# A block sum by accumulating DMA in the 7-product steps, in place of VectorE's add

## The chip, the cores and the metric

The kernel runs on one core of one Trainium2 chip. The metric is the device time of one execution in microseconds (us), median of several runs; smaller is better. A core has five engines with instruction streams of their own, each in order: TensorE (PE in the profile, its weight loads PEld), VectorE (DVE), ScalarE (ACT), GpSimd (POOL) and SyncE (SP). They meet only at semaphores. DMA transfers are issued by SP, ACT or POOL and carried out by 16 DMA engines.

## The reference

One layer of a hybrid block on x of 256 tokens by 4096 channels, all in float32. One input projection feeds two branches, sparse attention and a state-space mixer; each is projected back to 4096 channels, weighed by a sigmoid gate, summed, sent through an output projection, normalized and added to x. Cut to what matters:

```python
h = rms_norm(x, pre_norm_gain[layer])
proj = h @ w_in[layer]                      # 4096 x 24704
...
y_a = attn.reshape(b, s, ATTN_WIDTH) * jax.nn.silu(gate_a)
y_b = ssd_mixer(xs, z, bm, cm, dt_raw, ...)
gates = jax.nn.sigmoid(merge_logits.astype(jnp.float32)).reshape(b, s, N_BRANCHES, D_MODEL)
merged = (gates[:, :, 0, :] * (y_a @ w_branch_attn[layer])
          + gates[:, :, 1, :] * (y_b @ w_branch_ssd[layer]))
out = merged.astype(x.dtype) @ w_out[layer]
x = x + rms_norm(out, post_norm_gain[layer])
```

Nearly all work is in the matrix products with w_in, the two branch weights and w_out.

## The kernel before

**Float32 by three products.** Weights and activations are split into a rounded part and a rest (wh and wl, copy by ACT at L485, rest by VectorE at L487 or L489; both in `split`). `product` (L525) makes three matmuls of 128x128 by 128x512 (L532): rest times high, high times rest, high times high.

**Column pairs.** Most of the products run in `pair_gemm` (L514): two blocks of 512 output columns by two blocks of 128 tokens, over 4096 (or for the branches 2 x 2048) input channels in 16 steps of 256. A step loads 4 blocks of 128x512 weights in two raw tiles of two blocks each, ra and rb. A step of kind "S" computes its 2x2 block product with 7 products in place of 8 (Winograd's form), for which it needs sums and differences of the weight blocks; a step of kind "D" or "R" makes the 8 products. Which steps are S is set by the tables SX, SS, SY, SM: some 6 or 7 of 16. There are 172 S steps in all.

**One S step, before.** VectorE adds a block of rb to a block of ra (L580). `split(rb, 2)` gives b11, b21; `split(ra, 2)` gives t1 (the sum) and b22. VectorE then overwrites a block of ra with t2 (L585) and rb with t3, t4 (L586), and those are split too. ACT's copy and VectorE's rest of every tile alternate.

**What sets the order.** The program is written step by step; a scheduler puts each engine's instructions into an order by program position and its own estimate of times, so an instruction of a later step may stand ahead of one of an earlier step on the same engine. Raw tiles come from a pool of 8 (RBUFS), so the loads of a step wait until the tiles of the step four before it are free. wh and wl have 5 tiles each. Between the products, `step` (L106) lets generators in `aux` go on: evacuations of the pair before, attention, the state-space mixer, the forms of the next activations.

**The queues.** SP issues all weight loads (`load_half`, L145) and the loads of gates (sg, L1044). POOL issues 54 stores to scratch in DRAM: yscr (outputs of the two mixers, L763 and L946, 8 each), sscr (gates, L994, 32) and mscr (merged blocks, L1076, 6); and 28 loads of them as fr (L1001, L1006). ACT issues none.

The names: raw_N are the raw tiles, wh_N and wl_N the split parts, fr the reloaded activations, sg the reloaded gates, pc a pair's output in SBUF, p the PSUM banks.

Of the kernel before, what the change touches and what calls it, by code (L numbers as in the profile page):

```python
# [19 lines left out]
S = 256  # L20
# [14 lines left out]
SS = (1, 5, 8, 10, 12, 14)  # L35
SY = (1, 4, 6, 9, 12, 14)
SM = SX
GATES = [((n, br), (n + 1, br)) for n in (0, 2, 4, 6) for br in range(2)]
ISCALE = 32 ** -0.5 * 64 ** -0.5

# [5 lines left out]
def fused_block(tc, x, xT, w_qi, w_misc, w_q0, w_qk, w_vg, w_x, w_z, w_gate, w_br, w_out2, w_out,  # L46
# [467 lines left out]
    def pair_gemm(what, mode, chunk, plan, outs, evac, hooks={}, pace=1):  # L514
# [53 lines left out]

        after = max([n for n, (_, kind) in enumerate(plan) if kind == "S"], default=-2) + 1
        ended = []  # L570
        for n, (i, kind) in enumerate(plan):
            ra, rb = raw_tile(), raw_tile()
            load_half(ra, chunk(i), 0)
            load_half(rb, chunk(i), 1)
            if n in hooks:
                hooks[n]()
            assert kind_of[i] == what, (n, i, kind_of, len(aux))
            assert kind == "R" or ext_n[i] == {"S": 4, "D": 2}[kind], (n, i, ext_n)
            if kind == "S":
                V.tensor_add(ra[:, 0, :], ra[:, 0, :], rb[:, 0, :])  # L580
                b11, b21 = split(rb, 2)
                t1, b22 = split(ra, 2)
                if n == 1:
                    run_pending()
                V.tensor_sub(ra[:, 1, :], ra[:, 0, :], ra[:, 1, :])  # L585
                V.tensor_sub(rb, rb, ra[:, 1:2, :].to_broadcast([P, 2, NW]))  # L586
                t2, = split(ra[:, 1:2, :], 1)
                t3, t4 = split(rb, 2)
                now = {1: ("A11", b11), 2: ("A12", b21), 3: ("S4", b22), 4: ("A22", t4),
                       5: ("S1", t1), 6: ("S2", t2), 7: ("S3", t3)}  # L590
                for j in (2, 5, 3, 1, 6, 7, 4):
                    product(j, i, *now[j])
            else:
                w = {}
                w[1, 2], w[2, 2] = split(ra, 2, -1)
                w[1, 1], w[2, 1] = split(rb, 2)
                if n == 0 and len(pending) > 1 and turned[0] == "aux":
                    pending.pop(0)()
                if n == 1:
                    run_pending()  # L600
                if n == after:
                    early()
                    if not left.get(5):
                        late()
                        ended.append(5)
                if n == len(plan) - 1 and dest and not ended and left.get(8) == 0:
                    V.scalar_tensor_tensor(dest[3], dest[2], -1.0, ps[8], ALU.mult, ALU.subtract)
                    ended.append(8)
                todo = [(k, j) for j in ((5, 3, 2, 4) if kind == "D" else (3, 8, 2, 4))
                        for k in (1, 2)]  # L610
                for k, j in todo:
                    name = {2: f"A1{k}", 4: f"A2{k}", 8: f"A2{k}", 5: f"A2{k}",
                            3: f"D{k}" if kind == "D" else f"A1{k}"}[j]
                    product(j, i, name, w[k, 1 if j in (2, 4) else 2])
                    if (k, j) == todo[3]:
                        step(pace)
            step(pace)
# [82 lines left out]
    def attend(j, c):  # L700
# [59 lines left out]
            part(u)  # L760
            yield
        for i in range(2):
            nc.gpsimd.dma_start(yscr[2 * j + i], yraw[i].rearrange("p k t -> p (k t)"))  # L763

    push(make_rstd())
    for j in range(2):
# [156 lines left out]
    def finish(g, yvt):  # L923
        yv = [yvt[:, t, :] for t in range(2)]
        z = zs[g // 4]
        s2 = ssdp.tile([P, 2], F32, tag="ys2", name="ys2")
        for t in range(2):
            V.tensor_mul(yv[t], yv[t], z[2 * t + g % 4 // 2][:, g % 2 * S:g % 2 * S + S])
            sq = ssdp.tile([P, S], F32, tag="cacc", name="sq")
            A.activation(sq, yv[t], AF.Square, accum_out=s2[:, t:t + 1])  # L930
        ry = ssdp.tile([P, 2], F32, tag="yry", name="yry")
        rsqrt(ry, s2, 1.0 / S, ssdp)
        yield
        for t in range(2):
            A.activation(yv[t], yv[t], AF.Copy, scale=ry[:, t:t + 1])
        yield
        b = aux_bank().rearrange("p (c k) -> p c k", c=2)
        for c in range(2):
            for t in range(2):
                T.transpose(b[:, c, t * P:(t + 1) * P], yv[t][:, c * P:(c + 1) * P], ident)  # L940
        yb = ssdp.tile([P, 2, S], F32, tag="xd", name="yb")
        for c in range(2):
            k = 2 * g + c
            A.activation(yb[:, c, :], b[:, c, :], AF.Copy,
                         scale=pc[:, PC_NG + k:PC_NG + k + 1])
        nc.gpsimd.dma_start(yscr[8 + g], yb.rearrange("p k t -> p (k t)"))  # L946
        yield

    def ev_x(m):
# [39 lines left out]
    def ev_gate(cols):  # L989
        def run(c):  # L990
            for q, o in enumerate(c):
                t, (n, br) = q // 2, cols[q % 2]
                A.activation(o, o, AF.Sigmoid, scale=rstd[:, t:t + 1])
                nc.gpsimd.dma_start(sscr[br, n, t], o)  # L994
                if q % 2:
                    yield
        return run
# [48 lines left out]
    def ev_branch(n, br):  # L1046
        def run(c):
# [14 lines left out]
            for b in range(2):  # L1062
# [10 lines left out]
                    transpose4(c[2 * t + b], mT[:, :, t * P:(t + 1) * P], A)  # L1073
                    yield
                if n < 6:
                    nc.gpsimd.dma_start(mscr[n + b], mT.rearrange("p k t -> p (k t)"))  # L1076
                else:
                    for h in range(2):
                        merged[2 * (n + b) + h] = mT[:, 2 * h:2 * h + 2, :]
# [240 lines left out]
```

## Time and profile before

| | |
|---|---|
| median of 3 runs | 2861.69 us (2857.63 to 2864.1) |
| profiled execution, span from first to last instruction | 2848.7 us |
| median less span | 13.0 us |
| L580, the add in question | 172 times, 118.7 us |
| granted TensorE clock, mean | 0.996 |

The profiled execution is known by its span; its own device time isn't listed. The profile page gives busy time by engine, groups of instructions by line, and DMA issues. A row of a group reads: line, engine, operation, written tile <- read tiles, shapes, count | busy us, mean ns of one | idle us of the engine just before them, and what ended it. A row of the timeline reads: start us, length us, engine, line, operation, tiles, shape, count, and in brackets the idle time before it and what ended it. A "q" behind an engine's name means its instruction queue.

### The profile page before, as it was taken

Reading aid. Unit: us, or ns where it says so; the run is one execution under the profiler, and the core shown is the slowest. Engines: PE = TensorE matmul, PEld = TensorE weight load, DVE = VectorE, ACT = ScalarE, POOL = GpSimd, SP = SyncE. Lnnn points to the kernel's source line nnn. Section 1 sums busy time; section 2 is a strip of 40 time slices with the busy share of each in tenths; the row PEclk is TensorE's granted clock in tenths of the full one; section 3 lists DMA queues with packets and bytes.
Section 4 is the critical chain, followed back from the end, with each engine's and each line's share of the span. In section 5 each row is a group of like instructions: output and inputs, shape, how many; then the busy total and the mean of one; then the engine's idle time right before and its main releaser. Section 6 shows DMA issues by size and latency. Waiting matters only on the chain.

```text
span 2848.7 us, 35818 instructions
## 1 busy us (share of the span) xinstructions
PE 2813.4 (99%) x12744; PEld 2316.0 (81%) x12744; DVE 2407.6 (85%) x3039; ACT 1686.4 (59%) x2208; POOL 60.3 (2%) x98
## 2 busy tenths in 40 slices
PE   9999999999999999999999999999999999999997
PEld 7877888888888888888887788888887888888886
DVE  6668988989889878988898788988887899988875
ACT  7444565555656656876788555555555555555552
POOL 0100000000000000000000000000000000000000
PEclk9999999999999999999999999999999999999999
DMA  9544565655555555555555666666676676866673
GB/s 370 190 159 167 186 202 180 205 192 201 195 188 199 192 200 199 175 184 193 182 190 175 212 219 217 225 217 214 217 240 230 233 236 225 287 205 206 230 252 132
DMA packets 170852, 592.41 MB, mean 208 GB/s; under 512 B 19633, under 2 KB 20401, under 8 KB 170673
## 3 DMA queue, kind: packets, MB, share of 16 engines
q1 hardware_dynamic: 163728, 567.05, 58.6%
q0 software_dynamic: 6944, 23.07, 2.3%
q8 instruction: 100, 1.64, 0.2%
q14 instruction: 80, 0.65, 0.1%
HBM read 570.12 MB, written 19.92 MB: 207 GB/s over the span
## 4 chain that ended last, share of the span: by engine, by line
PE 55%; issue 35%; DVE 5%; DMA 3%; POOL 1%; ACT 0%; SPq 0%; POOLq 0%; DVEq 0%; ACTq 0%
PE p L532 43%; PE p L192 3%; PE p L193 3%; PE p L194 3%; DVE wl L489 1%; DVE wl L184 1%; PE p L362 1%; DMA fr<-yscr 1%; DMA raw<-w_out_d 1%; POOL sscr L994 0%; DMA raw<-w_qk_d 0%; DMA raw<-w_z_d 0%; PE p L393 0%; PE p L745 0%; DVE wl L487 0%
## 5 line engine op out<-in xcount | busy, mean ns | idle before, releaser
L485 ACT ACTIVATE wh<-raw 128x1024 fp32r<-128x1024 f32 (+1 forms) x1240 | 1186.3, 996 | 799.3 <-DVE raw L585 397.4
L532 PE MATMUL p<-wh,b 128*128 128x512 f32 x4504 | 1513.2, 393 | 3.6 <-ACT wh L485 1.8
L489 DVE TENSOR_TENSOR wl<-raw,wh 128x1024 fp32r<-128x1024 f32 (+1 forms) x964 | 1065.1, 1126 | 132.5 <-ACT wh L485 130.2
L532 PEld LDWEIGHTS p<-wh,b 128*128 128x128 f32 x4504 | 847.2, 188 | 179.1 <-ACT wh L485 4.1
L532 PE MATMUL p<-wl,b 128*128 128x512 f32 x2252 | 879.4, 391 | 6.1 <-DVE wl L489 3.8
L532 PE MATMUL p<-wh,ext 128*128 128x512 f32 x2320 | 810.5, 390 | 0.9 <-ACT wh L485 0.9
L532 PEld LDWEIGHTS p<-wh,ext 128*128 128x128 f32 x2320 | 435.6, 188 | 92.1 <-ACT wh L485 2.1
L532 PEld LDWEIGHTS p<-wl,b 128*128 128x128 f32 x2252 | 424.1, 188 | 93.6 <-DVE wl L487 4.8
L532 PE MATMUL p<-wl,ext 128*128 128x512 f32 x1160 | 452.7, 390 | 1.6 <-DVE wl L489 1.6
L487 DVE SCALAR_TENSOR_TENSOR wl<-raw,wh 128x1024 fp32r<-128x1024 f32 x276 | 337.0, 1221 | 48.0 <-ACT wh L485 47.7
L532 PEld LDWEIGHTS p<-wl,ext 128*128 128x128 f32 x1160 | 217.8, 188 | 50.9 <-DVE wl L489 5.7
L586 DVE TENSOR_TENSOR raw<-raw 128x1024 f32<-128x1024 f32 x172 | 210.5, 1224 | 3.8
L184 DVE TENSOR_TENSOR wl<-raw,wh 128x1024 fp32r<-128x1024 f32 x112 | 138.8, 1241 | 85.4 <-ACT wh L183 83.8
L192 PE MATMUL p<-wh,b 128*128 128x512 f32 x512 | 202.1, 396 | 1.7 <-ACT wh L180 1.7
L193 PE MATMUL p<-wl,b 128*128 128x512 f32 x512 | 200.1, 391 | 0.0
L194 PE MATMUL p<-wh,b 128*128 128x512 f32 x512 | 199.9, 391 | 0.0
L183 ACT ACTIVATE wh<-raw 128x1024 fp32r<-128x1024 f32 x112 | 118.4, 1060 | 131.1 <-PE p L194 118.4
L580 DVE TENSOR_TENSOR raw<-raw 128x512 f32<-128x512 f32 x172 | 118.7, 690 | 88.8 <-DMA raw<-w_gate_d 35.1
L585 DVE TENSOR_TENSOR raw<-raw 128x512 f32<-128x512 f32 x172 | 118.5, 689 | 2.3
L192 PEld LDWEIGHTS p<-wh,b 128*128 128x128 f32 x512 | 96.3, 188 | 26.0 <-ACT wh L180 3.3
L194 PEld LDWEIGHTS p<-wh,b 128*128 128x128 f32 x512 | 96.5, 189 | 20.4
L193 PEld LDWEIGHTS p<-wl,b 128*128 128x128 f32 x512 | 96.6, 189 | 19.9 <-DVE wl L181 0.4
(236 smaller groups left out, 1366.5 us busy)
## 6 DMA issues: line engine op xcount, KB each, us to landing
raw<-w_gate_d SPq DMA_DIRECT2D x256, 512.0 KB, 4.7
raw<-w_vg_d SPq DMA_DIRECT2D x128, 512.0 KB, 4.3
raw<-w_x_d SPq DMA_DIRECT2D x128, 512.0 KB, 4.3
raw<-w_br_d SPq DMA_DIRECT2D x128, 512.0 KB, 4.8
raw<-w_out_d SPq DMA_DIRECT2D x128, 512.0 KB, 4.7
raw<-w_qk_d SPq DMA_DIRECT2D x96, 512.0 KB, 4.5
raw<-w_z_d SPq DMA_DIRECT2D x64, 512.0 KB, 4.6
raw<-w_qi_d SPq DMA_DIRECT2D x62, 512.0 KB, 6.0
```

The lines of the kernel that those rows point to most:

```text
L183: A.activation(wh, rs, AF.Copy)
L184: V.tensor_sub(wl, rs, wh.bitcast(F32))
L192: T.matmul(ps[t], al[:, tk], wh[:, i, :], start=first, stop=False)
L193: T.matmul(ps[t], ah[:, tk], wl[:, i, :], start=False, stop=False)
L194: T.matmul(ps[t], ah[:, tk], wh[:, i, :], start=False, stop=last)
L485: A.activation(h, src, AF.Copy, scale=float(sign))
L487: V.scalar_tensor_tensor(l, src, -1.0, fbit(h), ALU.mult, ALU.subtract)
L489: V.tensor_sub(l, src, fbit(h))
L532: T.matmul(ps[j], l, r, start=first and n == 0, stop=left[j] == 0 and n == 2)
L580: V.tensor_add(ra[:, 0, :], ra[:, 0, :], rb[:, 0, :])
L585: V.tensor_sub(ra[:, 1, :], ra[:, 0, :], ra[:, 1, :])
L586: V.tensor_sub(rb, rb, ra[:, 1:2, :].to_broadcast([P, 2, NW]))
```

## The change

It takes the add out of VectorE and lets a DMA add: once ra is loaded, POOL issues a DMA that reads the block (the first block of rb) from DRAM a second time and accumulates it into ra. For this the loads of a step are written two steps ahead of its work (`fetch`, LEAD = 2). The stores of yscr, sscr and mscr move from POOL's queue to ACT's. Products and splits stay.

```diff
+LEAD = 2
...
-        for n, (i, kind) in enumerate(plan):
+        loaded = deque()
+
+        def fetch(n):
+            i, kind = plan[n]
             ra, rb = raw_tile(), raw_tile()
             load_half(ra, chunk(i), 0)
             load_half(rb, chunk(i), 1)
+            if kind == "S":
+                nc.gpsimd.dma_start(ra[:, 0, :], chunk(i)[:, HK, :], accum_op=ALU.add)
+            loaded.append((ra, rb))
+
+        for n in range(LEAD):
+            fetch(n)
+        for n, (i, kind) in enumerate(plan):
+            if n + LEAD < len(plan):
+                fetch(n + LEAD)
+            ra, rb = loaded.popleft()
...
             if kind == "S":
-                V.tensor_add(ra[:, 0, :], ra[:, 0, :], rb[:, 0, :])
                 b11, b21 = split(rb, 2)
                 t1, b22 = split(ra, 2)
...
-            nc.gpsimd.dma_start(yscr[2 * j + i], yraw[i].rearrange("p k t -> p (k t)"))
+            nc.scalar.dma_start(yscr[2 * j + i], yraw[i].rearrange("p k t -> p (k t)"))
...
-        nc.gpsimd.dma_start(yscr[8 + g], yb.rearrange("p k t -> p (k t)"))
+        nc.scalar.dma_start(yscr[8 + g], yb.rearrange("p k t -> p (k t)"))
...
-                nc.gpsimd.dma_start(sscr[br, n, t], o)
+                nc.scalar.dma_start(sscr[br, n, t], o)
...
-                    nc.gpsimd.dma_start(mscr[n + b], mT.rearrange("p k t -> p (k t)"))
+                    nc.scalar.dma_start(mscr[n + b], mT.rearrange("p k t -> p (k t)"))
```

The change moves instructions beyond these lines, since the scheduler orders anew. VectorE before, in the second gate pair; raw_13981 and raw_13982 belong to a D step, raw_14017 and raw_14018 to the S step after it, raw_14061 and raw_14062 to the next D step, raw_14097 and raw_14098 to the S step after that:

```order
L580 TENSOR_TENSOR raw_14097<-raw_14097,raw_14098 128x512
L489 TENSOR_TENSOR wl_13990<-raw_13982,wh_13989 128x1024
L489 TENSOR_TENSOR wl_14023<-raw_14018,wh_14022 128x1024
L489 TENSOR_TENSOR wl_14027<-raw_14017,wh_14026 128x1024
L585 TENSOR_TENSOR raw_14017<-raw_14017 128x512
L586 TENSOR_TENSOR raw_14018<-raw_14018,raw_14017 128x1024
L489 TENSOR_TENSOR wl_14033<-raw_14017,wh_14032 128x512
L489 TENSOR_TENSOR wl_14037<-raw_14018,wh_14036 128x1024
L487 SCALAR_TENSOR_TENSOR wl_14066<-raw_14061,wh_14065 128x1024
L489 TENSOR_TENSOR wl_14070<-raw_14062,wh_14069 128x1024
L489 TENSOR_TENSOR wl_14103<-raw_14098,wh_14102 128x1024
L489 TENSOR_TENSOR wl_14107<-raw_14097,wh_14106 128x1024
```

The add of one S step stands eleven rows ahead of the split of its sum, in front of the rest of three earlier steps. The same place of VectorE now (the tiles have other numbers: the two D steps are raw_13901, raw_13902 and raw_13990, raw_13991, the two S steps raw_13946, raw_13947 and raw_14026, raw_14027):

```order
L490 TENSOR_TENSOR wl_13999<-raw_13902,wh_13998 128x1024
L490 TENSOR_TENSOR wl_14032<-raw_13947,wh_14031 128x1024
L490 TENSOR_TENSOR wl_14036<-raw_13946,wh_14035 128x1024
L598 TENSOR_TENSOR raw_13946<-raw_13946 128x512
L599 TENSOR_TENSOR raw_13947<-raw_13947,raw_13946 128x1024
L490 TENSOR_TENSOR wl_14042<-raw_13946,wh_14041 128x512
L490 TENSOR_TENSOR wl_14046<-raw_13947,wh_14045 128x1024
L488 SCALAR_TENSOR_TENSOR wl_14075<-raw_13990,wh_14074 128x1024
L490 TENSOR_TENSOR wl_14079<-raw_13991,wh_14078 128x1024
L490 TENSOR_TENSOR wl_14112<-raw_14027,wh_14111 128x1024
L490 TENSOR_TENSOR wl_14116<-raw_14026,wh_14115 128x1024
```

The adds are gone, and VectorE's rows now follow the steps one after the other. POOL before, around the end of the state-space mixer (yb are its outputs, pc the gates):

```order
L994 DMA sscr_110<-pc_13454 128x512
L994 DMA sscr_110<-pc_13456 128x512
L946 DMA yscr_108<-yb_13844 128x512
L1001 DMA fr_17767<-yscr_108 128x512
L1001 DMA fr_17769<-yscr_108 128x512
L994 DMA sscr_110<-pc_14236 128x512
L994 DMA sscr_110<-pc_14233 128x512
```

and POOL now, at the same place:

```order
L580 DMA raw_13856<-w_gate_d 128x512
L580 DMA raw_13946<-w_gate_d 128x512
L1014 DMA fr_17776<-yscr_108 128x512
L1014 DMA fr_17778<-yscr_108 128x512
L580 DMA raw_14026<-w_gate_d 128x512
L580 DMA raw_14106<-w_gate_d 128x512
```

The stores have left, and accumulates stand before and behind the two loads of yscr. ACT now, at the head of a gate pair, with the stores among the gates' sigmoids (L1006) and the copies of the raw tiles (L486); before, its row held the four sigmoids one behind the other and no store:

```order
L1006 ACTIVATE pc_14899<-pc_14899,rstd_98 128x512
L1006 ACTIVATE pc_14897<-pc_14897,rstd_98 128x512
L1007 DMA sscr_110<-pc_14899 128x512
L1006 ACTIVATE pc_14896<-pc_14896,rstd_98 128x512
L486 ACTIVATE wh_14996<-raw_14931 128x512
L1007 DMA sscr_110<-pc_14896 128x512
L486 ACTIVATE wh_15000<-raw_14932 128x1024
L1007 DMA sscr_110<-pc_14897 128x512
```

Every store stands one to five rows behind the sigmoid that it stores.

## The prediction

> **What bounds the kernel now.** I read the page's busy times first, then the chain that ended last, then a table of stretches, then the groups of TensorE (PE), and last the timeline at the places where PE stood still.
>
> ```profile
> span 2848.7 us, 35818 instructions
> PE 2813.4 (99%) x12744; PEld 2316.0 (81%) x12744; DVE 2407.6 (85%) x3039; ACT 1686.4 (59%) x2208; POOL 60.3 (2%) x98
> ...
> PE 55%; issue 35%; DVE 5%; DMA 3%; POOL 1%; ACT 0%; SPq 0%; POOLq 0%; DVEq 0%; ACTq 0%
> ```
>
> PE is busy for 2813.4 of 2848.7 us, and the change removes no product. So the whole gain must come out of 35.3 us in which PE stands still. VectorE (DVE) at 85% is not the bound on the average; only where it is late for a moment does PE wait for it. The table of stretches tells where PE stands still (first number the length, second PE's busy time, fourth VectorE's, the fraction near the end the DMA engines' busy share):
>
> ```profile
> 290.00:1090.00 800.00, 797.68 (x3638) 659.68 (x3638) 703.44 (x830) 463.34 (x583) 4.46 (x8) 1.00 0.58 196
> 1090.00:1253.00 163.00, 162.43 (x761) 133.83 (x760) 144.22 (x208) 126.47 (x202) 1.09 (x2) 1.00 0.53 179
> 1253.00:1330.00 77.00, 75.16 (x343) 60.36 (x342) 65.96 (x98) 59.34 (x94) 1.09 (x2) 1.00 0.56 189
> 1330.00:1500.00 170.00, 169.58 (x780) 139.25 (x779) 151.97 (x206) 126.52 (x187) 1.08 (x2) 1.00 0.56 190
> 1500.00:1575.00 75.00, 72.76 (x337) 58.71 (x336) 65.37 (x103) 62.93 (x99) 2.17 (x4) 1.00 0.51 176
> 1575.00:1660.00 85.00, 79.87 (x348) 65.43 (x349) 68.97 (x82) 49.41 (x61) 4.36 (x8) 0.98 0.62 210
> 1660.00:2070.00 410.00, 410.00 (x1810) 339.46 (x1809) 355.57 (x370) 231.46 (x255) 10.84 (x20) 1.00 0.65 218
> 2070.00:2160.00 90.00, 87.27 (x376) 71.21 (x375) 74.70 (x108) 53.06 (x72) 9.36 (x18) 0.98 0.71 236
> 2160.00:2720.00 560.00, 559.73 (x2501) 463.20 (x2500) 485.03 (x561) 303.57 (x354) 10.35 (x19) 1.00 0.68 232
> ```
>
> These nine rows hold all column pairs. PE's idle time in them is 2.3 + 0.6 + 1.8 + 0.4 + 2.2 + 5.1 + 0 + 2.7 + 0.3 = 15.5 us; the other 20 us lie in the start and the tail, which the change doesn't touch. So **15.5 us is the ceiling**, 0.5% of the time. The groups say how much of it stands right before the products of the pairs (idle after the bar):
>
> ```profile
> L532 PE MATMUL p<-wh,b 128*128 128x512 f32 x4504 | 1513.2, 393 | 3.6 <-ACT wh L485 1.8
> L489 DVE TENSOR_TENSOR wl<-raw,wh 128x1024 fp32r<-128x1024 f32 (+1 forms) x964 | 1065.1, 1126 | 132.5 <-ACT wh L485 130.2
> L532 PE MATMUL p<-wl,b 128*128 128x512 f32 x2252 | 879.4, 391 | 6.1 <-DVE wl L489 3.8
> L532 PE MATMUL p<-wh,ext 128*128 128x512 f32 x2320 | 810.5, 390 | 0.9 <-ACT wh L485 0.9
> L532 PE MATMUL p<-wl,ext 128*128 128x512 f32 x1160 | 452.7, 390 | 1.6 <-DVE wl L489 1.6
> L580 DVE TENSOR_TENSOR raw<-raw 128x512 f32<-128x512 f32 x172 | 118.7, 690 | 88.8 <-DMA raw<-w_gate_d 35.1
> ```
>
> 3.6 + 6.1 + 0.9 + 1.6 = 12.2 us; the other 3.3 us stand before small products and transposes of the evacuations. The last row is the line that goes: 172 x 690 ns = 118.7 us of work, and 88.8 us in which VectorE stood in front of it and waited for a load.
>
> **What the removed add does today.** That waiting matters more than the 690 ns. The scheduler had put many of these adds ahead of work that belongs to earlier steps (the first pair of order pieces above): VectorE runs in order, so when the load is late, splits whose data has long been there wait behind the add. Three places, rows of VectorE, ScalarE (ACT) and PE:
>
> ```profile
> 1608.33 2.96 ACT L485 ACTIVATE wh<-raw 128x1024 fp32r<-128x1024 f32 x3 [0.98 <-PE p L532]
> 1614.91 0.69 DVE L580 TENSOR_TENSOR raw<-raw 128x512 f32<-128x512 f32 x1 [6.30 <-DMA raw<-w_gate_d]
> 1616.79 0.55 PE L532 MATMUL p<-wl,b 128*128 128x512 f32 x1 [2.88 <-DVE wl L489]
> ...
> 1572.75 0.69 DVE L580 TENSOR_TENSOR raw<-raw 128x512 f32<-128x512 f32 x1 [2.01 <-DMA raw<-w_gate_d]
> 1575.82 0.50 PE L532 MATMUL p<-wl,b 128*128 128x512 f32 x1 [1.21 <-DVE wl L487]
> ...
> 1263.45 0.69 DVE L580 TENSOR_TENSOR raw<-raw 128x512 f32<-128x512 f32 x1 [1.34 <-DMA raw<-w_x_d]
> 1266.86 0.50 PE L532 MATMUL p<-wl,ext 128*128 128x512 f32 x1 [0.31 <-DVE wl L489]
> 1268.53 0.50 PE L532 MATMUL p<-wl,ext 128*128 128x512 f32 x1 [0.69 <-DVE wl L489]
> ```
>
> At 1614.91 VectorE waited 6.30 us for a load that only a step further on needs; the wl that PE missed (wl_13990 in the order) had its wh from ACT by about 1609.4, the end of the first of the three copies that begin at 1608.33. Without the add in front it is done by about 1610.6, before PE needs it near 1613.9. These three places cost PE 2.88 + 1.21 + 0.31 + 0.69 = 5.1 us.
>
> **The change, part by part.**
>
> *The add goes from VectorE:* 5.1 us at the places above. Of the other 12.2 - 5.1 = 7.1 us, 2.7 us lie in the stretch 2070:2160, where the y forms wait for loads that have nothing to do with the add; they stay. Of the remaining 4.4 us I take half, since a queue that is 0.69 us per step shorter, and has no loads to wait for, helps where VectorE's split was what PE waited for, and not where ACT's was: 2.2 us. Together 7.3 us. Bounds: nothing (each stall finds another last wait) and 15.5 us.
>
> *The accumulate comes, 172 times, 256 KB each, on GpSimd's queue (POOL).* The trace before has no accumulating DMA. The nearest rows are POOL's loads of the same 128x512 size and SP's weight loads:
>
> ```profile
> L1001 POOL DMA_DIRECT2D fr<-yscr x16: 548/548/562, 1604.7 to 2159.1; - x16
> DMA to landing us min/median/max: 2.8/4.6/6.3
> ...
> L150 SPq DMA_DIRECT2D raw<-w_gate_d x256: 327/328/897, 1437.1 to 2120.5; - x128
> DMA to landing us min/median/max: 2.9/4.5/9.8
> ```
>
> I take 4.6 us from issue to landing, and keep 2.8 and, for a transfer that also reads its destination, 9.8 (SP's longest) as ends. What hides it: the time from the landing of ra to the moment when ACT first copies it. I measure that where a load is latest, the one that ended VectorE's wait at 1614.91:
>
> ```profile
> 1623.33 2.96 ACT L485 ACTIVATE wh<-raw 128x1024 fp32r<-128x1024 f32 x3 [0.21 <-ACT wh L485]
> 1624.48 3.49 DVE L489 TENSOR_TENSOR wl<-raw,wh 128x1024 fp32r<-128x1024 f32 x3
> ```
>
> In VectorE's order ra of that step (raw_14097) is the third of the three splits that begin at 1624.48, and ACT's copies run in the same order; the third of them begins near 1623.33 + 2/3 x 2.96 = 1625.3. Both halves were there by 1614.9, so over 10 us are free, against 4.6 needed (9.8 at the worst). So the accumulate's price is nothing as long as it lands within some 10 us; if that cover goes, each us beyond it holds up ACT's copy of ra, and behind it in ACT's and VectorE's order all later splits.
>
> The Trainium skill speaks against putting this on POOL: "SBUF — State Buffer", section "SBUF: two separate sides", says that GpSimd can't write a DMA's descriptors while VectorE runs an operation in a two-port mode, and its section "A bandwidth-pool intuition that's wrong" gives 3.1 us in place of 0.62 for such a DMA. By that the accumulate would land some 2.5 us later (an estimate from that page), 7.1 in place of 4.6. The rows above show no sign of it: POOL's issues last 548 to 562 ns each, with VectorE busy for 355.57 of 410 us in that stretch. The page's section "Who interferes with whom" also excludes tensor_tensor, the form of L489, from those modes.
>
> *More DMA work:* 172 x 256 KB = 45.1 MB, about 4.7% of the 16 engines' time by the page's row for SP's queue, twice that if the destination is read too:
>
> ```profile
> q1 hardware_dynamic: 163728, 567.05, 58.6%
> q0 software_dynamic: 6944, 23.07, 2.3%
> ```
>
> The fullest stretch (0.71) would reach about 0.80. Each 512 KB load may land up to 1 us later beside an accumulate; the 10 us cover takes that: nothing, at worst 2 us for the stretch after 1604, where sg loads already hold SP up.
>
> *54 stores move from POOL to ACT* (8 + 8 yscr, 32 sscr, 6 mscr). Such an issue on ACT isn't in the trace; SP's takes 0.33 us, POOL's 0.54. Each waits for ACT's own last result, for which this row of the waits is nearest (13.7 us in 23 times, 0.6 each):
>
> ```profile
> ACT wh L485 <- ACT wh L485: 13.7, 23, 1.0
> ```
>
> 54 x (0.33 + 0.6) = 50 us of ACT, in an engine that idles 179 of 410 us in the gate stretch: I take 1 us on the path, bounds 0 and 6. Some stores also wait for the semaphore of an older SP load; by the order those are loads about to be consumed, so they have landed. POOL loses 54 issues, and its loads of yscr and mscr now stand behind accumulates; an accumulate waits for its ra alone, which lands steps earlier than those loads are due: nothing.
>
> *Loads two steps ahead:* SP's order of loads is the same but for some neighbours changing places, and eight raw tiles still limit it to four steps. Nothing.
>
> **Sum.** -7.3 + 1 (ACT) + 0 = about -6.5 us in the span of 2848.7. The median of the runs, 2861.69, lies 13.0 us above that span; taking these 13.0 as unchanged, 2842.2 + 13.0 = **2855**. A measurement of this kernel tells about 0.2%, 5.7 us, from no change.
>
> **The rivals.**
> - *The stalls change owners.* PE has waits for ACT too (1.8 + 0.9 us in the groups), and ACT gets 50 us of stores, 32 of the 54 in bursts of four at the head of a gate pair. Against it: PE idles 0.0 us in 1660:2070. If it eats 6 of the 7.3: 2861.
> - *The accumulate is late (slower).* Place: ACT's copy of ra. It decides when landing takes over 10 us from ra's landing, three times POOL's shorter loads. If at one step in eight (21 of 172) 1 us is left after PE's lead, +21 - 6 = +15: 2876. For it: no row shows how long an accumulate lasts. Against it: 4.6 and 6.3 in the rows.
> - *All idle time before products goes*, the part in 2070:2160 too: -12.2 to -15.5, 2846 to 2850.
>
> **Chances.** Forecast (2851 to 2859) 0.52; owners change (2859 to 2864) 0.27; late accumulate 0.14; all gone 0.07. Faster by over 0.2% means below 2856.0: all of the last and about four fifths of the forecast, 0.48. Within: 0.35. Slower: the late accumulate and a little of the first rival, 0.17. The range for 8 in 10, 2846 to 2870, leaves out most of the late accumulate and a little below.
>
> **What would show it.** Right: no VectorE wait for a raw load of over 2 us in front of a split that PE waits for; PE's idle time in the nine stretches near 9 us, that of 1575:1660 near 2; accumulates landing in 3 to 7 us. Wrong: ACT waiting for the accumulate (the first rival's sign is ACT waiting for itself or a store's semaphore), or PE idle moved to the first steps of pairs.

## The result and the profile after

| | before | after |
|---|---|---|
| median of the first runs | 2861.48 us (2857.63 to 2864.1, 4 runs) | 2836.74 us (2835.93 to 2838.74, 4 runs) |
| ratio | | 0.9923, 95% interval 0.9908 to 0.9937 |
| span of the profiled execution | 2848.7 us | 2833.8 us |
| median on two other chips | 2850.8 and 2850.5 us | 2835.4 and 2835.8 us, ratio 0.9951 each (0.9938 to 0.9963, 0.9937 to 0.9964) |

Faster, by 24.7 us in the first runs, and by 15.4 and 14.7 us wherever the two were set side by side again. I had forecast 6.5 us and 2855 us, with a range of 2846 to 2870. The page of after, span and busy times:

```profile
span 2833.8 us, 36254 instructions
PE 2808.8 (99%) x12744; PEld 2314.6 (82%) x12744; DVE 2318.9 (82%) x2867; ACT 1693.3 (60%) x2210; POOL 179.8 (6%) x216
```

The spans differ by 14.9 us. PE's idle time went from 35.3 to 2833.8 - 2808.8 = 25.0 us, so 10.3 us came out of idle time. The other 4.6 us came out of PE's *busy* time, 2813.4 to 2808.8, with the same 12744 matmuls. The table of stretches of after, bounds shifted to the same products as the nine of before (first number the length, second PE's busy time, fourth VectorE's, near the end the DMA engines' share):

```profile
289.00:1086.00 797.00, 796.66 (x3638) 659.98 (x3637) 671.43 (x766) 465.36 (x583) 53.66 (x62) 1.00 0.72 217
1086.00:1249.00 163.00, 162.41 (x759) 133.70 (x758) 137.98 (x196) 126.52 (x202) 9.50 (x11) 1.00 0.64 195
1249.00:1325.50 76.50, 75.51 (x346) 61.18 (x346) 64.14 (x94) 59.51 (x94) 4.34 (x5) 1.00 0.67 204
1325.50:1495.00 169.50, 168.85 (x774) 137.95 (x773) 142.05 (x190) 123.57 (x184) 9.51 (x11) 1.00 0.66 205
1495.00:1568.00 73.00, 72.34 (x342) 59.69 (x341) 67.34 (x104) 63.70 (x101) 3.49 (x4) 1.00 0.65 194
1568.00:1646.00 78.00, 78.00 (x351) 64.67 (x350) 65.73 (x75) 53.35 (x64) 6.34 (x8) 1.00 0.83 257
1646.00:2056.00 410.00, 410.00 (x1810) 339.61 (x1809) 338.37 (x335) 233.89 (x255) 30.30 (x35) 1.00 0.79 241
2056.00:2147.00 91.00, 87.54 (x375) 71.09 (x375) 73.95 (x108) 54.06 (x72) 8.43 (x15) 0.98 0.74 238
2147.00:2706.60 559.60, 559.47 (x2499) 462.99 (x2498) 466.59 (x526) 303.27 (x355) 37.51 (x48) 1.00 0.79 249
```

PE idles 0.3 + 0.6 + 1.0 + 0.7 + 0.7 + 0 + 0 + 3.5 + 0.1 = 6.8 us here, against 15.5. The largest piece is 5.1 to 0 in the stretch that held the wait at 1614; the y forms' stretch went from 2.7 to 3.5.

Where busy time was lost is seen in two stretches of before behind that wait (the column ahead of the DMA share is the granted clock):

```profile
1616.00:1618.00 2.00, 1.21 (x3) 0.96 (x4) 2.00 (x3) 0.00 (x0) 0.00 (x0) 0.78 0.09 27
1618.00:1620.00 2.00, 2.00 (x6) 1.61 (x5) 1.93 (x3) 0.15 (x1) 0.00 (x0) 0.50 0.70 240
```

and in one of after at the same products:

```profile
1604.00:1606.00 2.00, 2.00 (x11) 1.65 (x10) 1.97 (x3) 1.04 (x2) 0.89 (x1) 1.00 0.99 350
```

At half clock a 2 us stretch holds 6 matmuls in place of 11, and PE counts as busy. So a wait can cost more than its idle time: with 0.78, 0.50 and 0.87 granted in 1616 to 1622, this one cost 2 x (0.22 + 0.50 + 0.13) = 1.7 us more (my estimate from the clock). It doesn't follow every time, as the last section shows.

The waits tell more than PE's own rows. ScalarE in front of its copies, in the table of waits of before (us in total, times, longest):

```profile
ACT wh L485 <- DVE raw L585: 397.4, 125, 8.6
ACT wh L485 <- PE p L532: 260.7, 239, 2.6
```

and of after:

```profile
ACT wh L486 <- PE p L533: 443.0, 358, 2.6
ACT wh L486 <- DVE raw L598: 216.3, 90, 6.7
```

L585, now L598, is VectorE's subtraction inside an S step. Before, ScalarE stood 397 us waiting for it: VectorE was late, and I read from it that the splits ran just ahead of PE. After, ScalarE waits most for PE to give back a wh buffer: the splits run ahead until the five buffers are full more often. Such a lead covers small delays. The row tells that VectorE is late, not what that costs, as experiment 7 shows.

The accumulates in the view of their line after: issues of the gate pairs, then for all 172 who waited for them (us, times) and the time to landing:

```profile
L580 POOL DMA_DIRECT2D raw<-w_gate_d x50: 857/866/891, 1442.2 to 2059.1; - x50
...
  ACT wh L486: 6.5, 2
...
DMA to landing us min/median/max: 3.6/5.8/9.3
```

and the software and ScalarE queues on the page of after:

```profile
q0 software_dynamic: 27008, 52.44, 10.5%
q10 hardware_dynamic: 7776, 15.73, 1.5%
```

They land in 5.8 us in the median, and only 2 of 172 copies waited for one, 6.5 us in all. My estimate by the Trainium skill's "SBUF — State Buffer" (section "A bandwidth-pool intuition that's wrong") was 7.1 us and by POOL's loads 4.6; the trace lies between and doesn't decide. Queue 0 went from 2.3% to 10.5% though the 54 stores (1.5%) left it: about 9.7% for the accumulates, the upper of my two figures.

### The profile page after: what moved, and what is told of

Read it like the earlier page. It is cut to its first block, busy times and chain, and to the rows that moved or that the text cites. A ratio compares the mean times of both kernels' runs of the same rounds, so it can differ in the third digit from the quotient of the medians.

```text
span 2833.8 us, 36254 instructions
## 1 busy us (share of the span) xinstructions
PE 2808.8 (99%) x12744; PEld 2314.6 (82%) x12744; DVE 2318.9 (82%) x2867; ACT 1693.3 (60%) x2210; POOL 179.8 (6%) x216
## 3 DMA queue, kind: packets, MB, share of 16 engines
q0 software_dynamic: 27008, 52.44, 10.5%
## 4 chain that ended last, share of the span: by engine, by line
PE 89%; DVE 5%; issue 3%; DMA 2%; ACT 1%; SPq 0%; POOL 0%; DVEq 0%; ACTq 0%; POOLq 0%
PE p L533 74%; PE p L193 4%; PE p L194 4%; PE p L195 4%; DVE wl L490 1%; PE p L363 1%; ACT wh L486 1%; DMA fr<-yscr 1%; PE p L890 0%; DVE raw L599 0%; DMA raw<-w_x_d 0%; DVE wl L185 0%; PE p L758 0%; PE p L725 0%; PE p L394 0%
## 5 line engine op out<-in xcount | busy, mean ns | idle before, releaser
L486 ACT ACTIVATE wh<-raw 128x1024 fp32r<-128x1024 f32 (+1 forms) x1240 | 1190.9, 995 | 775.3 <-PE p L533 443.0
L490 DVE TENSOR_TENSOR wl<-raw,wh 128x1024 fp32r<-128x1024 f32 (+1 forms) x964 | 1064.1, 1125 | 242.8 <-ACT wh L486 237.7
L195 PE MATMUL p<-wh,b 128*128 128x512 f32 x512 | 199.3, 389 | 0.0
L598 DVE TENSOR_TENSOR raw<-raw 128x512 f32<-128x512 f32 x172 | 118.6, 689 | 3.8
L195 PEld LDWEIGHTS p<-wh,b 128*128 128x128 f32 x512 | 96.1, 188 | 20.1
L580 POOL DMA_DIRECT2D raw<-w_gate_d x50 | 43.3, 867 | 587.5 <-DMA raw<-w_gate_d 280.2
```

The lines of the kernel that those rows point to most:

```text
L195: T.matmul(ps[t], ah[:, tk], wh[:, i, :], start=False, stop=last)
L486: A.activation(h, src, AF.Copy, scale=float(sign))
L490: V.tensor_sub(l, src, fbit(h))
L580: nc.gpsimd.dma_start(ra[:, 0, :], chunk(i)[:, HK, :], accum_op=ALU.add)
```

## The experiments

Each time is a median, on the chip of its set, beside the kernel before on that same chip. The kernel before had medians of 2848.8 to 2850.8 us on six chips.

**1. The level: both kernels unchanged** (e1_before, e7_after, e15_after_again).

> The kernel before, unchanged, to see the span and the granted clock of several executions beside their times. After the change a run's time lies 2.1 us above its span. Theory A: the same holds before, so the executions timed at 2857 to 2864 us have spans of 2855 to 2862, and the profiled one (2848.7) was a quicker one, by 6 to 13 us; then the gain of 24.7 us between the medians is all within the span, and the profile of before shows too few or too short stalls. Rival B: the time outside the span is 13 us before and 2 after (spans near 2848.7 at times near 2861.5), and 10 us of the gain lie outside what the trace shows.

> The changed kernel, unchanged, beside the kernel before on the same chip, since on the chip of the last four runs the kernel before took 2850.7 us and not 2861.5. Theory A (the gain is that of the two spans on record, 2848.7 - 2833.8 = 14.9 us, and the rest of the 24.7 was the chip of the first runs): 12 to 17 us under the kernel before of these runs. Rival B (it is 20 us or more on every chip): 0.993 of before or less.

> The changed kernel once more beside the kernel before. The first result had 24.7 us between the medians, the pair of runs since then 15.4, with the changed kernel the same in both (2836.7 and 2835.4) and the kernel before not (2861.5 and 2850.8). Theory A (it is the chip or the time of the first runs, in which the kernel before had longer stalls): 14 to 17 us again on the same chip, 20 or more perhaps on another. Rival B (the difference is chance between executions of one chip): single executions of the kernel before between 2857 and 2864 us turn up here too.

A run's time lies 2.1 to 2.5 us above its span before and 2.1 to 2.3 after, so B of the first falls: the gain doesn't lie outside the span. In the six sets the kernel before took 2843.7 to 2858.1 us in 99 executions, and only one was over 2857, where all four of the first runs lay. Side by side the gain is 15.4 and 14.7 us. What made the first four of before 10 us longer, with after the same, stays open: of those four no spans are listed, and no later chip showed it.

**2. The sum in its turn** (e2_add_in_turn), before with (`behind[-1]` is the last split of the step before)

```diff
-                V.tensor_add(ra[:, 0, :], ra[:, 0, :], rb[:, 0, :])
+                with tc.issue_after(behind[-1]):
+                    V.tensor_add(ra[:, 0, :], ra[:, 0, :], rb[:, 0, :])
```

> The kernel before with one edit: each block sum stays on VectorE, but is issued behind the last split of the step before it (172 of 172 in turn, where before 162 stood ahead of 1 to 7 splits of earlier steps). VectorE's work is the same, 118.7 us of sums. Theory A (the place of the sum in VectorE's queue costs, by waits for its load in front of splits, and by the slower clock after them): at least two thirds of the gain of 24.7, so 2835 to 2845 us. Rival B (the 118.7 us of work cost): within 5 us of before, 2856 to 2863 us.

2863.9 against 2850.7 us, ratio 1.005 (1.0038 to 1.0062): **13 us slower**, against both theories. The sum's group in this kernel:

```profile
L586 DVE TENSOR_TENSOR raw<-raw 128x512 f32<-128x512 f32 x172 | 117.6, 684 | 0.0
```

and a row of its table of waits:

```profile
ACT wh L486 <- DVE raw L586: 147.6, 99, 5.8
```

VectorE's wait for loads is gone (0.0, where it was 88.8), and ScalarE now waits 147.6 us for the sum. The early place in the queue, which I had taken for the fault, was the better of the two places tried.

**3. The other edits.** After without its accumulate and with VectorE's sum (e6_lead_only). Its 54 stores stay on ScalarE's queue, though the expectation below says GpSimd's, so it is the kernel before with the loads ahead and the moved stores:

```diff
-            if kind == "S":
-                nc.gpsimd.dma_start(ra[:, 0, :], chunk(i)[:, HK, :], accum_op=ALU.add)
...
+                V.tensor_add(ra[:, 0, :], ra[:, 0, :], rb[:, 0, :])
```

before with the 54 stores on ScalarE's queue (e4_stores_only), and after with them back on GpSimd's (e3_stores_on_pool, the same lines the other way):

```diff
-                nc.gpsimd.dma_start(sscr[br, n, t], o)
+                nc.scalar.dma_start(sscr[br, n, t], o)
```

> The kernel before with the loads taken two steps ahead in the code and nothing else: sums stay on VectorE, stores on GpSimd. My prediction's term was nothing, as the order of loads is the same: within 4 us of the kernel before. Rival (loads ahead carried part of the gain): 6 us or more under it.

> The kernel before with the 54 stores moved from GpSimd's queue to ScalarE's and nothing else. Undoing this in the changed kernel gave 2837.5 in place of 2835.4 us. Theory A (nothing either way): within 4 us of the kernel before. Rival (the stores held up something on GpSimd's queue, or cost ScalarE): 6 us or more off, either way.

> The changed kernel with one edit undone: the 54 stores are back on GpSimd's queue. My prediction's term for them was +1 us on ScalarE (0 to 6). Theory A (stores cost ScalarE about that, and gain nothing): 2833 to 2837 us, at or below the changed kernel's 2836.7. Rival B (the stores behind accumulates on GpSimd's queue come late, and moving them was part of the gain): 2842 us or more.

Loads ahead and stores: 2852.8 against 2850.8, 1.001 (1.0002 to 1.0019). Stores alone: 2855.0 against 2850.5, 1.0014 (1.0005 to 1.0024), 1.4 to 6.8 us slower, a little more than the 4 us of the theory. Stores back: 2837.5 against 2850.7, 0.9959 (0.9947 to 0.9971), the same as the changed kernel's 0.9951. None of them carries gain. Loads ahead had no run alone; e6 beside e4 shows no cost and no gain of them. The stores cost a little with the sum on VectorE, and nothing that shows without it. And e6 differs from the changed kernel in the sum alone: 2852.8 against 2835.4 us on the same chip, 17 us for the exchange.

**4. No sum at all** (e5_no_add), before with

```diff
-                V.tensor_add(ra[:, 0, :], ra[:, 0, :], rb[:, 0, :])
```

> The kernel before without the sum of the two blocks at all (its products come out wrong by that sum, all else is done): no VectorE work, no accumulate, stores and loads as before. Theory A (the accumulates are hidden and cost nothing): 2833 to 2839 us, the same as the changed kernel within 4 us. Rival B (the accumulates cost something by load times): 2830 us or less. Rival C (loads two steps ahead or the moved stores carried the gain): 2845 us or more.

2834.7 against 2850.7, 0.9948 (0.9937 to 0.996), 16.0 us less. This kernel leaves the sum out, so it shows what the sum costs in all. The changed kernel's 0.9951 is the same within the interval, about 1 us above it: the accumulates are hidden.

**5. Work and wait put back into the changed kernel** (e8_work_only, e9_wait_only), with a two-element tile `dum`:

```diff
+    dum = const.tile([P, 2], F32, name="dum")
...
+                    V.tensor_reduce(dum, ct[:, None, 0:S].to_broadcast([P, 2, S]), AX.X, ALU.add)
```
```diff
+                V.tensor_copy(dum, rb[:, 0, 0:2])
```

> The changed kernel plus one VectorE operation of some 0.6 to 0.7 us in each of the 172 steps that had the sum, a reduction of 512 elements of a constant, in turn behind the last split of the step before: VectorE's work as before, but nothing that waits for a load and nothing that waits for it. Theory A (the 118.7 us of work were the cost, by VectorE being late with the splits): 10 us or more above the changed kernel. Rival B (the wait for the load in front of other splits was): within 4 us of the changed kernel. Rival C (the chain from load to sum to ScalarE's copy was): also within 4 us, told from B by the next run.

> The changed kernel plus a copy of two elements of rb on VectorE where the sum stood: it takes some 0.1 us, but waits for the step's second load, and 162 of the 172 stand ahead of 1 to 7 splits of earlier steps, as the sums did before. Theory A (the work was the cost): within 4 us of the changed kernel, 0.06 to 0.1 us for each copy being 10 to 17 us of VectorE's time at most. Rival B (the wait in front of splits): 8 us or more above the changed kernel, and VectorE idle in front of these copies for about 90 to 100 us.

2873.9 and 2872.9 against 2850.8: 38 us over the changed kernel, both alike. Neither is what was asked. PE hardly idles in them, yet from start to start a product takes 230.3 ns on average in place of 227.1. The tile had moved base, raw, wh and wl by 32 bytes; a run with that alone follows.

**6. The shift alone** (e13_shift_only), the changed kernel with

```diff
+    dum = const.tile([P, 2], F32, name="dum")
+    V.memset(dum, 0.0)
```

> The changed kernel with a two-element tile more, written once at the start: it moves the tiles base, raw, wh and wl by 32 bytes (their addresses are then 32 and not 0 modulo 64), and nothing else. Theory (PE's pace hangs on where its operands lie): 2871 to 2875 us, 37 us above the changed kernel, with PE at 230.2 ns a product on average. Rival (the slow pace came from the work or the wait of the first try): within 3 us of the changed kernel.

2868.8 us, 33 us above the changed kernel, 2 us under the range of the theory and far from the rival's. PE's groups with ext of this kernel:

```profile
L535 PE MATMUL p<-wh,ext 128*128 128x512 f32 x2320 | 823.4, 395 | 0.1
L535 PE MATMUL p<-wl,ext 128*128 128x512 f32 x1160 | 459.4, 396 | 0.7 <-DVE wl L492 0.7
```

and of after:

```profile
L533 PE MATMUL p<-wh,ext 128*128 128x512 f32 x2320 | 810.4, 390 | 0.0
L533 PE MATMUL p<-wl,ext 128*128 128x512 f32 x1160 | 452.6, 390 | 0.6 <-DVE wl L490 0.2
```

The mean of one grows from 390 to 395 ns. From start to start it is again 230.3 ns in place of 227.1 on average over all products, and 11808 of them make 37 us, a little more than the 33 us measured.

**7. Work and wait put back, addresses moved by 256 bytes**: the work (e10_work_aligned, held behind the last split of the step before) and the wait (e11_wait_aligned) by the lines of 5, both together (e14_wait_and_work) with a shorter reduction that nothing holds in place:

```diff
+    dum = const.tile([P, 64], F32, name="dum")
...
+                V.tensor_copy(dum[:, 0:2], rb[:, 0, 0:2])
+                V.tensor_reduce(dum[:, 0:2], ct[:, None, 0:192].to_broadcast([P, 2, 192]), AX.X, ALU.add)
```

> The run with VectorE's work put back (a reduction of 512 constant elements, 0.68 us, 172 times, in turn), once more: in the first try the two-element result tile had moved base, raw, wh and wl by 32 bytes, and PE took 230.25 ns a product in place of 227.12 on average, 37 us for 11808 products, which hid what was asked. Here the tile has 64 elements, so all addresses move by 256 bytes. PE's pace is to be 227.1 ns. Theory A (VectorE's time is the cost, by splits that come late): 10 us or more above the changed kernel's 2835.4. Rival B (the wait for the load in front of other splits) and rival C (ScalarE's copy waiting for the sum): within 4 us of it.

> The run with the wait put back (a copy of two elements of rb, 162 of 172 ahead of 1 to 7 splits of earlier steps), once more with the 64-element tile, so that addresses move by 256 bytes and PE's pace is 227.1 ns. In the first try VectorE stood 105.1 us in front of these copies and they took 28.3 us themselves. Theory A (VectorE's time is the cost, and 28 us of it is a quarter of the sum's): 2 to 5 us above the changed kernel's 2835.4. Rival B (the wait in front of splits is the cost): 8 us or more above it.

> The changed kernel with both put back at once: the two-element copy of rb where the sum stood (0.17 us each, waits for the load ahead of other splits) and behind it a reduction of 384 constant elements (some 0.52 us), together about the sum's 118.7 us of VectorE, with nothing that waits for them; addresses move by 256 bytes. Theory A (the sum costs by its work and by its wait, and the two add up: 6.5 us for the work alone and 8.4 for the wait alone with 28 us of work): 2848 to 2853 us, the time of the kernel before. Rival B (the two overlap, and what is left is ScalarE's copy of ra waiting for the sum): 2841 to 2845 us.

PE's pace is 227.2 ns in all three. The work alone: 2841.8 against 2848.8, 0.9972 (0.9962 to 0.9982). The wait alone: 2843.7, 0.9984 (0.9975 to 0.9992). Both: 2858.6 against 2850.5, 1.0035 (1.0022 to 1.0048). The added operation of the work alone:

```profile
L601 DVE TENSOR_REDUCE dum<-ct 128x2 f32<-128x512 f32 x172 | 116.7, 679 | 0.0
```

of the wait alone:

```profile
L595 DVE COPY dum<-raw 128x2 f32<-128x2 f32 x172 | 28.6, 166 | 102.9 <-DMA raw<-w_gate_d 45.0 <-DMA raw<-w_out_d 23.4 <-DMA raw<-w_br_d 14.6
```

and the copy where both are back:

```profile
L595 DVE COPY dum<-raw 128x2 f32<-128x2 f32 x172 | 28.7, 167 | 122.1 <-DMA raw<-w_gate_d 56.1 <-DMA raw<-w_out_d 25.5 <-DMA raw<-w_br_d 12.6
```

Set against the changed kernel's ratio of 0.9951, work costs 0.0021 or 6 us, the wait 0.0033 or 9 us, both 0.0084 or 24 us, each give or take some 5. The first tries of 5, set against e13 with the same addresses, give 5 and 4 us. Either counts, so the rivals that give one of them nothing fall. But both together cost more than the sum itself (14 us by the same ratio), against A and B.

In e10 ScalarE waits nearly as long for VectorE as in the kernel before (397.4 us there), yet e10 is 7 us faster:

```profile
ACT wh L488 <- DVE raw L606: 392.2, 138, 7.5
```

**8. The same without accumulates**, on the kernel before. Wait and work with no result (e16_dose_no_accumulate): the two lines of e14 in place of the sum. Wait and result (e18_small_sum):

```diff
-                V.tensor_add(ra[:, 0, :], ra[:, 0, :], rb[:, 0, :])
+                V.tensor_add(ra[:, 0, 0:2], ra[:, 0, 0:2], rb[:, 0, 0:2])
```

Wait and result, with the reduction of e14 written behind the small sum (e17_small_sum_and_work). All three leave out the sum or all but two of its 512 columns.

> The kernel before with the sum left out and in its place the same two VectorE operations as in the run before last: a two-element copy of rb that waits for the load, and a reduction of 384 constant elements; no accumulates, stores on GpSimd's queue, loads as before. With accumulates this took 2858.6 us, 8 over the kernel before. Theory A (the accumulates' traffic makes the weight loads land later, which costs only where VectorE waits for them): 2846 to 2853 us, the time of the kernel before. Rival B (work and wait cost 23 us whatever the traffic, and the sum itself less for another reason): 2855 us or more.

> The kernel before with the sum cut to its first two elements, still written to ra, so that ScalarE's copy of ra waits for it as before, and the rest of its work as a reduction of 384 constant elements behind it; no accumulates. The run with the same two operations but the small one written to a tile that nobody reads took 7.1 us less than the kernel before. Theory A (the missing half of the cost is that ScalarE's copy of ra waits for the sum): 2847 to 2853 us, the time of the kernel before. Rival B (it is not; the work itself differs, a sum of two tiles against a reduction): 2839 to 2844 us.

> The same without the reduction: wait and result as before, but 0.17 us of work in place of 0.69. Theory A (work costs 5 to 7 us of the 15, as the run with the work alone said): 2841 to 2846 us. Rival B (work costs nothing, wait and result all): 2847 to 2853 us, the time of the kernel before. Rival C (work is all): 2833 to 2838 us.

| VectorE has in an S step | accumulates | less the kernel before | ratio, interval |
|---|---|---|---|
| nothing (e5) | no | -16.0 us | 0.9948, 0.9937 to 0.996 |
| wait, result, 0.16 us (e18) | no | -8.3 us | 0.9971, 0.9959 to 0.9982 |
| wait, work, no result (e16) | no | -7.1 us | 0.9976, 0.9966 to 0.9986 |
| wait, result, 0.16 us; the work ran before the pairs (e17) | no | +1.6 us | 1.0007, 0.9998 to 1.0016 |
| nothing (after: e7, e15) | yes | -15.4, -14.7 us | 0.9951 |
| work (e10) | yes | -7.0 us | 0.9972 |
| wait (e11) | yes | -5.1 us | 0.9984 |
| wait, work (e14) | yes | +8.1 us | 1.0035 |

e17 has the kernel before's time, as its theory A said, but not for A's reason. Nothing waits for its reduction and it waits for nothing, so the scheduler put all 172 of them at the start of the program, ahead of the first S step. The view of their line (length in ns, then the first and the last start in us):

```profile
L582 DVE TENSOR_REDUCE dum<-ct x172: 533/546/555, 20.4 to 238.8; 128x2 f32<-128x384 f32 x172
```

In e16, where they write the tile that the copy has just written, they lie among the S steps, as meant:

```profile
L582 DVE TENSOR_REDUCE dum<-ct x172: 535/546/555, 290.9 to 2719.2; 128x2 f32<-128x384 f32 x172
```

The 94 us hold up the start: in the profiled executions (spans 2847.7 and 2839.5 us) the 1365th matmul, near the first pair, begins at 300.1 us in e17 and at 289.3 in e18. From there to the end the two take 2547.6 and 2550.2 us. So what e17 takes longer than e18, 9.9 us in the medians, arises before the pairs; that e17 meets the kernel before is chance, and it says nothing of how wait, result and work share the sum's cost.

What stands: without its sum the kernel takes 16.0 us less, and e18, which keeps 26.8 of the 118.7 us of work (and waits 82.4 us), takes 8.3 less. So 92 us of work are worth about half, somewhat more than e18's theory A allowed. e16 has wait and work and also keeps only half of the cost, below both its theories; its result goes nowhere, and it waits 72.0 us in place of 88.8. What the result costs and what the wait costs beside it isn't settled. ScalarE's direct wait for the sum is small (6.9 us in 5 times, before).

The wait in front of the added operation without accumulates, e16, to be read beside the 122.1 us of e14 above:

```profile
L581 DVE COPY dum<-raw 128x2 f32<-128x2 f32 x172 | 28.1, 163 | 72.0 <-DMA raw<-w_out_d 20.3 <-DMA raw<-w_gate_d 14.5 <-DMA raw<-w_br_d 11.8
```

The same two operations wait 72.0 us in e16 and 122.1 in e14, and cost 15 us less. That looks like the accumulates' doing, but e14 also has the loads ahead and the stores on ScalarE's queue. In e6, with these two and no accumulate, the sum waits as long:

```profile
L592 DVE TENSOR_TENSOR raw<-raw 128x512 f32<-128x512 f32 x172 | 118.2, 687 | 118.5 <-DMA raw<-w_gate_d 55.4 <-DMA raw<-w_out_d 22.6 <-DMA raw<-w_br_d 16.7
```

The stretch of some 410 us that holds most of the gate pairs (from the 7571st matmul to the 9381st) tells more. VectorE's waits for its loads there, in e16 (1650.7 to 2060.9 us), e14 (1656.8 to 2073.8), e4 with the stores alone (1655.4 to 2071.7) and e6 (1654.2 to 2071.0), in this order:

```profile
DVE dum L581 <- DMA raw<-w_gate_d: 10.4, 15, 1.6
...
DVE dum L595 <- DMA raw<-w_gate_d: 43.7, 25, 4.1
...
DVE raw L580 <- DMA raw<-w_gate_d: 43.0, 25, 3.2
...
DVE raw L592 <- DMA raw<-w_gate_d: 45.6, 25, 3.4
```

These products take 410.2, 417.0, 416.3 and 416.8 us, and 410.3 both in the kernel before and in the changed one. With the copy alone (e11) they take 412.0. So 6 to 7 of the 15 us arise where VectorE has such a wait and as much work and the stores stand on ScalarE's queue, with accumulates or without. What makes the rest is open.

Whether accumulates delay the weight loads is better seen in e6 and after, which differ in the sum and its accumulate alone. The median landing of the loads in the seven groups that have accumulates moves by -0.3 to +0.7 us, and is later in six of them. The largest difference, e6 and then after:

```profile
raw<-w_x_d SPq DMA_DIRECT2D x128, 512.0 KB, 4.0
...
raw<-w_x_d SPq DMA_DIRECT2D x128, 512.0 KB, 4.7
```

That this costs nothing in the changed kernel fits with VectorE having no operation left that waits for a load in front of earlier splits; no run tests it by itself.

**9. The sum on GpSimd's cores** (e12_gpsimd_sum), before with

```diff
-                V.tensor_add(ra[:, 0, :], ra[:, 0, :], rb[:, 0, :])
+                G.tensor_add(ra[:, 0, :], ra[:, 0, :], rb[:, 0, :])
```

> The kernel before with the sum of the two blocks computed by GpSimd in place of VectorE: no accumulate and no loads ahead. It tells whether the gain needs a DMA or only that the sum leaves VectorE. Theory A (leaving VectorE is enough, GpSimd being 2% busy): within 4 us of the changed kernel, 2833 to 2840 us. Rival (GpSimd's sum is late, as it waits for loads and takes longer, and ScalarE's copy waits for it, or it slows VectorE): 2845 us or more.

2864.8 against 2848.8, 1.0056 (1.0042 to 1.007): slower. The sum on GpSimd, and two VectorE groups of this kernel, whose mean before was 1126 ns (L489) and 686 ns (L585, in e1_before):

```profile
L580 POOL TENSOR_TENSOR raw<-raw 128x512 f32<-128x512 f32 x172 | 323.6, 1881 | 1926.1 <-DMA raw<-w_gate_d 406.8 <-DMA raw<-w_x_d 276.7 <-DMA raw<-w_vg_d 243.8
L489 DVE TENSOR_TENSOR wl<-raw,wh 128x1024 fp32r<-128x1024 f32 (+1 forms) x964 | 1139.4, 1205 | 169.9 <-ACT wh L485 166.5 <-DMA raw<-w_out_d 0.8
...
L585 DVE TENSOR_TENSOR raw<-raw 128x512 f32<-128x512 f32 x172 | 140.1, 814 | 3.8
```

The sum takes 1881 ns in place of 690, and VectorE's operations with two inputs grow: 79 ns x 964 + 128 ns x 172 = 98 us in these two groups. With the others VectorE is busier than before, 2454.1 us in place of 2407.6, though the 118.7 us of the sum have left it:

```profile
PE 2819.6 (98%) x12744; PEld 2315.4 (81%) x12744; DVE 2454.1 (86%) x2867; ACT 1683.6 (59%) x2209; POOL 383.9 (13%) x270
```

The Trainium skill's "SBUF — State Buffer", section "Who interferes with whom", gives a reason: a VectorE instruction with two inputs in SBUF contends with a GpSimd instruction that reads SBUF. The trace agrees: L585, with two inputs, grows from 686 to 814 ns. In the changed kernel, whose sums are DMAs, L490 stays at 1125 ns.

## Why the prediction was wrong

- **The level, the step "taking these 13.0 as unchanged", failed.** The 13 us between the profiled span and the median were no distance that each run has; that is 2.1 to 2.5 us. So the profiled execution must have been a shorter one than those timed, and the gain in the medians of the first runs was 10 us more than that of the spans. Of the 18.5 us between 2855.2 and 2836.7, 10.1 come from this step and 8.4 from the size of the next term. That the changed kernel came out at 2836.7 in the first runs and 2835.4 later, while the kernel before fell from 2861.5 to 2850.8, is not explained.
- **The mechanism was right in its direction, the term for the sum's going was mis-sized.** I gave it 7.3 us: 5.1 for three places and "half" of 4.4 for a queue shorter by 0.69 us a step. It measured 16.0 us (no sum at all). Its work alone is worth 6 us put back (e10) and 8.3 for 92 of the 118.7 us taken out (e18), where I had 2.2 for all that lies outside the three places. "That waiting matters more than the 690 ns" isn't borne out: e18 keeps most of the wait (82.4 of 88.8 us) and yields half of the gain by the work alone, and the wait alone measured 9 and 4 us.
- **The three places**: the longest wait went, as forecast, and with it the half clock behind it, which my 5.1 us left out; the idle time of its stretch went from 5.1 to 0.
- **The ceiling of 15.5 us** was not one in principle. It held for idle time (8.7 of 15.5 us went in the nine stretches), but 4.6 us of the 14.9 came out of busy time. That the spans' 14.9 us lie just under it is luck.
- **The view I did not read** was ScalarE's wait for L585, 397 us in 125 waits over 172 S steps: VectorE was late in most of them. PE's idle time shows where its lead ran out in one execution, not how thin it was elsewhere. But the row is a sign and no price: e10 has 392 us of it and half of the gain.
- **Right:** the accumulate costs nothing (about 1 us over no sum at all); it landed in 5.8 us against an estimate of 4.6 with ends of 2.8 and 9.8, and only 2 copies of ScalarE waited for one. Loads ahead: nothing that shows. Stores: +1 forecast with bounds 0 and 6, 1.4 to 6.8 with the sum on VectorE and nothing visible beside the accumulates. The 2.7 us of the y forms stayed (3.5). Weight loads landed at most 0.7 us later in the median, where I allowed 1. No VectorE wait for a raw load over 2 us is left. Of the rivals, neither "the stalls change owners" nor "late accumulate" happened.

## What to carry to other kernels

Where one engine paces and the engines before it feed it just in time, work taken from a feeder can be worth more than the pacing engine's idle time suggests: here 16 us, where I took 7.3 from 12.2 us of idle time. Look also at what waits for the feeder over all steps; it tells that the feeder is late, though not what that costs. An accumulating DMA takes a sum away entirely, work, wait and result; moving the sum in the queue or to GpSimd's cores made this kernel slower. When a probe adds an operation that nothing depends on, look in its trace where the operation ran, and when two probes differ in three things, look for runs that differ in one. Before a profiled span and a median are put into one sum, look whether they are of the same executions.

## What the runs showed of the hardware that I had not expected

**32 bytes of address cost 1.2%.** With base, raw, wh and wl at 32 modulo 64 in place of 0, products with ext took 395 ns in place of 390 and the kernel 33 us more; a shift by 256 bytes left the pace at 227 ns. Not every product slows: those of wl and b in the pairs took 389 ns in place of 390, and those of the start (L195 to L197 in e13) stayed at 389 to 394. Which operand it is was not tried. A tile added for a probe can hide what the probe asks.

**The half clock comes after short waits, and not always.** A wait of PE in the timeline of after, and the stretch behind it:

```profile
2142.42 0.59 PE L533 MATMUL p<-wh,b 128*128 128x512 f32 x1 [1.90 <-DVE pc L548]
```
```profile
2144.00:2146.00 2.00, 2.00 (x6) 1.52 (x5) 2.00 (x4) 2.00 (x3) 0.08 (x1) 0.50 0.40 136
```

and a wait of the same length in e1_before, with its stretch:

```profile
1614.88 0.50 PE L532 MATMUL p<-wl,b 128*128 128x512 f32 x1 [1.91 <-DVE wl L489]
```
```profile
1616.00:1618.00 2.00, 2.00 (x11) 1.64 (x10) 1.93 (x3) 0.07 (x1) 0.00 (x0) 1.00 0.71 242
```

1.90 us were followed by a clock of 0.50, 1.91 us were not. Likewise 1.76 us in e15 were, and 1.75 us in e7 were not. The Trainium skill's "TensorE: Matmul & The Clock Gate" ("Part 1: The HAM clock gate (the "warmup" mystery)") lets the clock halve after at least one idle window of about 3.4 us, the windows running freely. That it doesn't follow every time agrees; that 1.90 us of idle PE were enough once does not.
